# Decoder trunk on one core: the second attention's scores as three float32r products, its splits tied behind the copies, bias and maximum in one pass

## The chip, the core and the metric

The kernel runs on one core of a Trainium2 chip. The metric is device time in microseconds (us), the median of several executions; smaller is better. TensorE is called PE here (PEld is its weight load), VectorE DVE, ScalarE ACT, GpSimd POOL, and SP is the engine whose queue issues nearly all DMAs.

## The reference, cut to what matters

One sequence of 256 tokens, width 1024, 16 heads of 64. Layer 0 is a dilated sliding-window attention (three dilations), layer 1 is a forgetting attention, each followed by a SwiGLU block with a hidden width of 2816; all in float32. The change is mostly in the forgetting attention:

```
q, k, v, log_f = split(h @ w_in)          # log_f: one forget gate per head and token
c = cumsum(log_sigmoid(log_f + b_f))      # along the sequence
s = (q @ k.T) * 64 ** -0.5 + c_i - c_j    # per head, queries in two blocks of 128
s = where(key <= query, s, -1e30)
o = softmax(s) @ v
out = o @ w_out
```

## The kernel before

**Big products.** Every float32 weight and activation is split into two float32r halves: a high half made by a copy on ACT (`split`, line 74) and a low half made by a subtraction on DVE (line 78). `mm3` (lines 197 and 202) then forms a product as high x high, high x low and low x high, three float32r matmuls into one PSUM bank. Weights come in pieces: `piece` loads 128x2048 floats in two raw tiles of 128x1024 (five such buffers, issued on SP at line 95), and each raw tile costs one ACT copy (tile `wh`) and one DVE subtraction (tile `wl`). `weights(nm, i)` emits the pieces up to two ahead of the one that it returns; a raw buffer is free again when both of its halves are made.

**Order.** The program is written out as one long list. The framework orders each engine's queue ahead of time, by priority and by its own model of when inputs are ready; `first()` raises the priority of what is inside, and `tc.issue_after(ins)` places an instruction behind `ins` in its engine's queue. At run time each engine takes its queue strictly in order, and waits on semaphores.

**First attention.** The loop over `a_units` makes q and k of each dilation by `proj_feat`, and `rotated` (lines 433 to 436) turns them on DVE: a shuffle, a product with `rcos` that is the last read of the PSUM bank (line 434, returned as `read`), a product with `rsin`, a sum. In unit 2, before `rotated`, the code asks for `weights("a_in", 1)`, computes half of the next unit ahead of time, and scales `rcos` and `rsin` (line 569).

**Second attention.** `b_units` lists 12 weight units: three values first, then for four head quads `hq` the units q (`w = 0`) and k (`w = 1`), and the last quad's values. The loop's iterations 3 to 11 run them. Iteration i asks for its weights, which emits the splits of the unit two further on; it runs `proj_feat` for two halves (`c = 0, 1`), 24 matmuls of 256 columns each; then ACT copies the result from PSUM to SBUF, scaled by 0.125 for q (line 939, tile `fb`). PSUM tiles come in pairs (tags `mm`, `sc`, `tr`, `o`, two banks each).

Hooks in `due` put the attention of a quad between the halves of later units. After the k unit of quad `hq` (iterations 4, 6, 8, 10), `scores_b(hq, 0)` runs after the first half of the next iteration and `scores_b(hq, 1)` after its second. For a pair of heads, each on its own 64 array rows (`own`), `scores_b` issues four plain float32 matmuls (line 855; two query blocks of 128 and 256 keys for each head), on DVE one addition of the bias (line 861, 384 columns a head) and two maxima (line 865, 128 and 256 columns), on ACT an exponential for each (line 283), then a reciprocal (line 870) and the scaling by it, on ACT (line 872) and DVE (line 873). `trans_b` transposes the result on PE and copies it on DVE (line 297); `pv_b` multiplies by the values (line 304). `bias` (lines 838 to 841) fetches a bias tile by DMA and adds the causal mask on POOL. The low halves of the pieces that iterations 3 and 5 emit are collected in `behind` and released behind the gate scan or the first scores' addition.

Of the kernel before, what the change touches and what calls it, by code (L numbers as in the profile page):

```python
# [31 lines left out]
def trunk(ctx: ExitStack, tc: tile.TileContext, T, out):  # L32
# [10 lines left out]
    def first():  # L43

        return tc.high_priority(offset=300)
# [22 lines left out]
    euler = cst.tile([P, 1], F32, name="euler")  # L68
    nc.gpsimd.memset(euler, math.e)

    def split(pair, view, src, early=True, after=None):
        hi, lo = pair
        with first() if early else nullcontext():
            a = nc.scalar.activation(view(hi), src, AF.Copy)  # L74

            def low(after=None):
                with tc.issue_after(after.ins) if after else nullcontext():
                    return nc.vector.tensor_tensor(view(lo), src, view(hi).bitcast(F32), op=ALU.subtract)  # L78

            if isinstance(after, list):  # L80
                return after.append(low)
            return a, low(after)


    def piece(key, todo=None):
        if key[0][:2] == "dn" and key[1] == LATE:
            wh, wl = (y.rearrange("p k c -> p (k c)") for y in fm_tile("ot", KT, 1))
        else:
            wh, wl = (wp.tile([P, WIDE], F32R, tag=y, name=y, bufs=4) for y in ("wh", "wl"))
        if key == GATED:  # L90
            wh, wl = (y.rearrange("p (k c) -> p k c", k=KT) for y in (wh, wl))
        for c in range(2):
            raw = wp.tile([P, 1024], F32, tag="raw", name="raw", bufs=5)
            u = slice(c * 1024, (c + 1) * 1024)
            nc.sync.dma_start(raw, T[key[0]][key[1]][:, u])
            view = lambda y, u=u: y[:, u]
            if key == GATED:
                raw = raw.rearrange("p (k c) -> p k c", c=256)
                view = lambda y, c=c: y[:, c * 4:c * 4 + 4, :256]
            cut = lambda after=None, raw=raw, view=view: split((wh, wl), view, raw, False, after)  # L100
            if todo is None:
                cut()
            else:
                todo.append(cut)
        if key == GATED:
            cut = lambda after=None: split((wh, wl), lambda y: y[:, :, 256:], wf32, False, after)
            todo.append(cut)
        return wh, wl

# [35 lines left out]
    ready = {}  # L145
    state = {"next": 0}

    def weights(nm, i, after=None, ahead=AHEAD):

        upto = order.index((nm, i)) + ahead  # L150
        while state["next"] <= min(upto, len(order) - 1):
            key = order[state["next"]]
            cuts = []
            ready[key] = piece(key, cuts)
            for cut in cuts:
                cut(after)
            state["next"] += 1
        return ready.pop((nm, i))

# [122 lines left out]
    def exps(s, nm, den, j):  # L282
        nc.scalar.activation(s, s, AF.Exp, bias=nm[:, j:j + 1], accum_out=den[:, j:j + 1])
# [5 lines left out]
    def transposed(blocks, copy=nc.vector.tensor_copy, tag="tr"):  # L289

        tr = psum(tag)
        for i, b in enumerate(blocks):
            nc.tensor.transpose(tr[:, i * P:(i + 1) * P], b, ident)  # L293
        n = len(blocks) * P
        w = ap.tile([P, 512], F32, tag="pt", name="pt", bufs=3)
        with first():
            copy(w[:, :n], tr[:, :n])
        return w

    def pv(o, v, kb, pr, w, n, start, stop):  # L300

# [223 lines left out]
    def later(i, fn, *a):  # L525
        due.setdefault(i, []).append((fn, a))

    quads = [{"hq": hq, "fm": {}, "pt": {}, "v": {}} for hq in range(4)]
    for i, (hq, g, w) in enumerate(a_units):
        quad = quads[hq]  # L530
        if i == 3:
            o = o_next
        elif i:

            wt = weights("a_in", hq * 9 + g * 3 + w, read if i > 4 else None)
        if i != 3 and (w < 2 or g == 0 and hq > 1):
            o = psum("mm")
        if i == 1:
            ident = const("ident", [P, P])
            rcos = const("rcos", [P, S])  # L540
            rsin = const("rsin", [P, S])
        if i == 2:
            mask0 = const("mask0", [P, 3 * P])
            mask12 = const("mask12", [P, S])
        if i in (24, 31):
            x.append(hrow("x"))
            t = len(x) - 1
            nc.sync.dma_start(x[t], T["x"][t * P:(t + 1) * P, :])
        if w < 2:
            for c in range(2):  # L550
                if i == 3 and c == 0:
                    continue
                proj_feat(xt, wt, o[:, c * S:(c + 1) * S], c, (KT // 2, rstd_a) if i == 2 and c == 1 else None)
            if i == 2:
                values_12(quad["v"], lead)

                wt = weights("a_in", 1)
                o_next = psum("mm")
                rb = psum("tr")

                def rows():
                    for t in range(2):
                        nc.tensor.matmul(rb[:, t * P:(t + 1) * P], r_a[t].to_broadcast([P, P]), ident,
                                         start=True, stop=True)

                proj_feat(xt, wt, o_next[:, :S], 0, (6, rows))
                with first():
                    for c in (rcos, rsin):
                        nc.vector.tensor_tensor(c, c, rb[:, :S], op=ALU.mult)
            q, read = rotated(o, g, w)  # L570
            quad["fm"][g, w] = q
            if w == 1:

                j = i + (hq == 0)
                if g == 0:
                    for pr in range(2):
                        later(j + 2 + pr, scores_a, quad, g, pr)
                else:
                    later(j + 3 - g, scores_a, quad, g)
                if g == 2:  # L580
                    later(j + 1, softmax_a, quad)
                    j = 9 * hq + 11 + 2 * (hq == 0)
                    for pr in range(2):
                        later(j + pr, trans_a, quad, pr)
                        later(j + 1 + pr, pv_a, quad, pr)
        elif g == 0 and hq > 1:
            for t in range(2):
                proj_tok(xt, wt, o[:, t * S:(t + 1) * S], t)
            quad["v"][0] = v_tile(o, r_a)
        elif i > 1:  # L590


            half = hq % 2 if g == 0 else g - 1
            if half == 0:

                lead = [psum("mm" if g else "o") for _ in range(2)]
            proj_pair(xt, wt, lead, half)
            if half and g == 0:
                vs = [v_tile() for _ in range(2)]
                for t in range(2):  # L600
                    v_pair(vs, lead[t], t, r_a[t])
                for y in range(2):
                    quads[hq - 1 + y]["v"][0] = vs[y]
            elif half:
                values_12(quad["v"], lead)
        for fn, a in due.pop(i, ()):
            fn(*a)
# [239 lines left out]
    def scores_b(hq, pr):  # L847
# [3 lines left out]
        pt = b.setdefault("pt", {})  # L851
        scs = [psum("sc") for _ in range(2)]
        for qb in range(2):
            for h in range(2):
                last = nc.tensor.matmul(scs[h][:, qb * P:qb * P + (qb + 1) * P], b[0][own[h], pr, qb * P:(qb + 1) * P],  # L855
                                        b[1][own[h], pr, :(qb + 1) * P], start=True, stop=True)
        for h in range(2):
            s = p_tile()
            with first():
                bias_h = b["bias", pr][:, h * 3 * P:(h + 1) * 3 * P]  # L860
                added = nc.vector.tensor_tensor(s[:, :3 * P], scs[h][:, :3 * P], bias_h, op=ALU.add)
            for qb in range(2):
                j = h * 2 + qb
                sv = s[:, qb * P:qb * P + (qb + 1) * P]
                nc.vector.tensor_reduce(nm[:, j:j + 1], sv, axis=AX.X, op=ALU.max, negate=True)
                exps(sv, nm, den, j)
            pt[pr, h] = s
        release(added)
        c = stat_tile("c_b", 4)
# [49 lines left out]
    for hq in range(2):  # L919
        for pr in range(2):  # L920
            later(3 + 2 * hq, bias, hq, pr)
    for i, (hq, w) in enumerate(b_units):
        if i < 3:
            continue
        wt = weights("b_in", hq * 3 + w, behind if i in (3, 5) else None)
        o = psum("mm")
        if w < 2:
            for c in range(2):
# [4 lines left out]
            if w == 0:  # L933

                for fn, a in due.pop(i, ()):
                    fn(*a)
            bq[hq][w] = ap.tile([P, 2, S], F32, tag=f"fm{w}", name=f"fb{w}", bufs=2)
            with first():
                nc.scalar.activation(bq[hq][w], o.rearrange("p (a b) -> p a b", a=2), AF.Copy, scale=(0.125, 1.0)[w])
            if w == 1:  # L940
                j = i + 1

# [150 lines left out]
```

## Time and profile before

| | |
|---|---|
| median of 3 runs | 751.36 us (750.59 to 751.94) |
| the profiled execution | 752.26 us |
| its span, and what lies around it | 750.5 us, 1.76 us |
| granted TensorE clock | 0.997 |
| busy DVE, ACT, POOL | 500.7, 373.7, 67.3 us |
| bytes read by DMA | 136.07 MB, 183 GB/s over the span |

The second attention's loop lies at about 467 to 535 us of the span. In the lines of the profile, a group's row gives line, engine, operation, tiles, shape and count, then the total busy time in us and the mean of one instruction in ns, then the idle time of the engine before them. A timeline row gives start and duration in us; several instructions in a row are merged, and their number stands behind the x. A PE duration contains the pipeline's fill, so the pace of matmuls is read from start to start.

### The profile page before, as it was taken

How to read it: one execution, taken by the hardware profiler on the slowest of the kernel's cores; microseconds unless marked ns; L12 is line 12 of the kernel's file. 1: busy time of each engine (PE TensorE's matmuls, PEld its weight loads, DVE VectorE, ACT ScalarE, POOL GpSimd, SP SyncE). 2: the span in 40 equal slices, each digit the busy share in tenths (PEclk: the TensorE clock that was granted, in tenths of full speed). 3: DMA queues.
4: the chain of work that ended last, by engine and by line, in shares of the span. 5: the costliest groups of instructions: out<-in, count | busy, mean ns of one | idle time of the engine just before them, and what ended most of it. 6: DMA issues, size and time to landing. Idle time of an engine off the chain costs nothing.

```text
span 750.5 us, 14329 instructions
## 1 busy us (share of the span) xinstructions
PE 740.2 (99%) x5916; PEld 680.1 (91%) x5916; DVE 500.7 (67%) x752; ACT 373.7 (50%) x617; POOL 67.3 (9%) x98
## 2 busy tenths in 40 slices
PE   9999999999999999999999999999999999999996
PEld 7998989999998789999999988989889999999995
DVE  6987978876879376554556365799867545456533
ACT  7635537437427365444445355467556444445521
POOL 0600004004004000000000004312000000000001
PEclk9999999999999999999999999999999999999998
DMA  9865544645646267656567543784537665656601
GB/s 332 302 195 170 169 142 156 210 142 169 198 133 200 88 225 242 204 179 205 181 198 250 169 129 127 268 252 155 166 95 235 217 205 179 199 193 213 210 1 56
DMA packets 39441, 138.07 MB, mean 184 GB/s; under 512 B 4528, under 2 KB 5840, under 8 KB 39376
## 3 DMA queue, kind: packets, MB, share of 16 engines
q1 hardware_dynamic: 39232, 137.01, 55.3%
q8 instruction: 46, 0.75, 0.4%
q14 instruction: 19, 0.16, 0.1%
q10 hardware_dynamic: 144, 0.15, 0.1%
HBM read 136.07 MB, written 1.07 MB: 183 GB/s over the span
## 4 chain that ended last, share of the span: by engine, by line
PE 93%; ACT 2%; DVE 2%; DMA 2%; issue 1%; SPq 0%; POOL 0%; POOLq 0%; DVEq 0%; ACTq 0%
PE ps_mm L202 32%; PE ps_mm L197 17%; PE ps_tr L202 9%; PE ps_sc L202 8%; PE ps_o L202 7%; PE ps_tr L197 5%; PE ps_sc L197 4%; PE ps_o L197 4%; PE ps_o L304 2%; PE ps_tr L293 1%; DMA otl<-in_lead 1%; PE ps_sc L450 1%; PE ps_sc L466 1%; PE ps_sc L855 1%; ACT wh L74 1%; DMA raw<-in_a_in 1%
## 5 line engine op out<-in xcount | busy, mean ns | idle before, releaser
L74 ACT ACTIVATE wh<-raw 128x1024 fp32r<-128x1024 f32 x236 | 243.0, 1054 | 247.5 <-PE ps_mm L202 85.8
L78 DVE TENSOR_TENSOR wl<-raw,wh 128x1024 fp32r<-128x1024 f32 x236 | 287.7, 1238 | 81.8 <-ACT wh L74 81.5
L197 PE MATMUL ps_mm<-xt,wh 128*128 128x256 f32 x816 | 228.2, 280 | 0.7 <-DVE qk L434 0.7
L202 PE MATMUL ps_mm<-xt,wl 128*128 128x256 f32 x816 | 226.3, 277 | 0.1
L202 PE MATMUL ps_mm<-xt,wh 128*128 128x256 f32 x816 | 226.2, 277 | 0.0
L197 PEld LDWEIGHTS ps_mm<-xt,wh 128*128 128x128 f32 x816 | 153.3, 188 | 4.4 <-issue 3.3
L202 PEld LDWEIGHTS ps_mm<-xt,wl 128*128 128x128 f32 x816 | 153.4, 188 | 0.5 <-DVE wl L78 0.5
L202 PEld LDWEIGHTS ps_mm<-xt,wh 128*128 128x128 f32 x816 | 153.7, 188 | 0.0
L202 PE MATMUL ps_tr<-xt,wl 128*128 128x256 f32 x304 | 83.9, 276 | 0.0
L202 PE MATMUL ps_tr<-xt,wh 128*128 128x256 f32 x304 | 83.9, 276 | 0.0
L197 PE MATMUL ps_tr<-xt,wh 128*128 128x256 f32 x304 | 83.7, 276 | 0.0
L692 DVE TENSOR_TENSOR sa<-ps_tr,sa 128x256 f32<-128x256 f32 x38 | 16.1, 424 | 74.1 <-PE ps_tr L202 74.0
L202 PEld LDWEIGHTS ps_tr<-xt,wl 128*128 128x128 f32 x304 | 57.1, 188 | 0.0
L202 PEld LDWEIGHTS ps_tr<-xt,wh 128*128 128x128 f32 x304 | 57.1, 188 | 0.0
L197 PEld LDWEIGHTS ps_tr<-xt,wh 128*128 128x128 f32 x304 | 56.9, 188 | 0.0
L279 POOL COPY v<-v 32x256 f32<-32x256 f32 x64 | 36.1, 563 | 180.3 <-ACT v L275 177.6
L197 PE MATMUL ps_mm<-wh,xt 128*128 128x512 f32 (+1 forms) x144 | 50.1, 348 | 0.0
L202 PE MATMUL ps_mm<-wl,xt 128*128 128x512 f32 (+1 forms) x149 | 49.3, 336 | 0.0
L202 PE MATMUL ps_mm<-wh,xt 128*128 128x512 f32 (+1 forms) x149 | 49.2, 335 | 0.0
L167 POOL TENSOR_SCALAR rs<-ssq 128x1 f32<-128x1 f32 x7 | 2.1, 307 | 425.2 <-ACT junk L176 425.2
L197 PE MATMUL ps_sc<-wh,ah 128*128 128x512 f32 x80 | 31.4, 392 | 0.0
L202 PE MATMUL ps_sc<-wl,ah 128*128 128x512 f32 (+1 forms) x82 | 31.3, 385 | 0.0
(224 smaller groups left out, 1112.9 us busy)
## 6 DMA issues: line engine op xcount, KB each, us to landing
raw<-in_gu SPq DMA_DIRECT2D x88, 512.0 KB, 4.8
raw<-in_a_in SPq DMA_DIRECT2D x68, 512.0 KB, 4.4
raw<-in_dn SPq DMA_DIRECT2D x44, 512.0 KB, 4.5
raw<-in_b_in SPq DMA_DIRECT2D x24, 512.0 KB, 5.0
raw<-in_a_out SPq DMA_DIRECT2D x8, 512.0 KB, 4.5
raw<-in_b_out SPq DMA_DIRECT2D x8, 512.0 KB, 4.9
bias<-sums SPq DMA_DIRECT2D x8, 384.0 KB, 6.3
grow<-in_norms SPq DMA_DIRECT2D x4, 512.0 KB, 5.4
```

The costliest lines, as they stand in the source:

```text
L74: a = nc.scalar.activation(view(hi), src, AF.Copy)
L78: return nc.vector.tensor_tensor(view(lo), src, view(hi).bitcast(F32), op=ALU.subtract)
L167: nc.gpsimd.tensor_scalar(m, s, rest, None, op0=ALU.add)
L197: nc.tensor.matmul(o, sh, mh, start=start, stop=False)
L202: last = nc.tensor.matmul(o[:, u], s, m[:, u], start=False, stop=end and u.stop == n)
L279: nc.gpsimd.tensor_copy(v[1 + a % 2][n:n + 32, a // 2 * S:a // 2 * S + S], by_t[a * 32:a * 32 + 32, t, g])
L293: nc.tensor.transpose(tr[:, i * P:(i + 1) * P], b, ident)
L304: nc.tensor.matmul(o[h * HD:(h + 1) * HD], v[:, c:c + HD], w(h), start=start, stop=stop)
L450: nc.tensor.matmul(scs[h][:, qb * P:qb * P + (qb + 1) * P], q[hr[h], pr, qb * P:(qb + 1) * P], k[hr[h], pr, :(qb + 1) * P], start=True, st ...
L466: nc.tensor.matmul(sc[h][c, o:o + 64], q[hr[h], pq, qb * P + a * 32:qb * P + a * 32 + 32], k[hr[h], pq].rearrange("p (b n) -> p b n", b=2) ...
L692: nc.vector.tensor_tensor(a, u, sg, op=ALU.mult)
L855: last = nc.tensor.matmul(scs[h][:, qb * P:qb * P + (qb + 1) * P], b[0][own[h], pr, qb * P:(qb + 1) * P], b[1][own[h], pr, :(qb + 1) * P], ...
```

## The change

It does four things.

1. `scores_b` takes q and k as pairs of float32r halves. The ACT copy after each q and k unit now writes the high half; a new DVE instruction (`scalar_tensor_tensor`, 128x512, from PSUM and the high half) writes the low half into a tile `low` of the tag `h`. Each of the four score products becomes three float32r matmuls over 64 rows (high x high, high x low, low x high), alternating between the two heads.
2. The addition of the bias and the two maxima of a head become two `tensor_tensor_reduce`, of 128 and 256 columns, which write the negated sum and its minimum; the exponential runs with scale -1.
3. The pieces that iteration i of the second attention's loop emits are tied, in ACT's and DVE's queues, behind the ACT copy and the DVE low half of iteration i - 1 (`held`).
4. In unit 2 of the first attention, the second of the two low halves of `weights("a_in", 1)` is tied behind `read` of that unit's `rotated`.

```diff
+    def behind_(ins):
+        return tc.issue_after(ins.ins) if ins else nullcontext()
+
-    def split(pair, view, src, early=True, after=None):
+    def split(pair, view, src, early=True, after=None, hold=None):
         hi, lo = pair
         with first() if early else nullcontext():
-            a = nc.scalar.activation(view(hi), src, AF.Copy)
+            with behind_(hold and hold[0]):
+                a = nc.scalar.activation(view(hi), src, AF.Copy)
...
             if isinstance(after, list):
                 return after.append(low)
-            return a, low(after)
+            return a, low(after or hold and hold[1])
...
-    def weights(nm, i, after=None, ahead=AHEAD):
+    def weights(nm, i, after=None, ahead=AHEAD, hold=None):
...
-                cut(after)
+                cut(after, hold)
...
+    PRODUCTS = ((0, 0), (0, 1), (1, 0))
...
-                wt = weights("a_in", 1)
+                second = []
+                wt = weights("a_in", 1, second)
+                second.pop(0)()
...
             q, read = rotated(o, g, w)
+            if i == 2:
+                second.pop()(read)
...
         for qb in range(2):
-            for h in range(2):
-                last = nc.tensor.matmul(scs[h][:, qb * P:qb * P + (qb + 1) * P], b[0][own[h], pr, qb * P:(qb + 1) * P],
-                                        b[1][own[h], pr, :(qb + 1) * P], start=True, stop=True)
+            for i, (y, z) in enumerate(PRODUCTS):
+                for h in range(2):
+                    last = nc.tensor.matmul(scs[h][:, qb * P:qb * P + (qb + 1) * P],
+                                            b[0][y][own[h], pr, qb * P:(qb + 1) * P],
+                                            b[1][z][own[h], pr, :(qb + 1) * P], start=i == 0, stop=i == 2)
         for h in range(2):
             s = p_tile()
-            with first():
-                bias_h = b["bias", pr][:, h * 3 * P:(h + 1) * 3 * P]
-                added = nc.vector.tensor_tensor(s[:, :3 * P], scs[h][:, :3 * P], bias_h, op=ALU.add)
+            bias_h = b["bias", pr][:, h * 3 * P:(h + 1) * 3 * P]
             for qb in range(2):
-                j = h * 2 + qb
-                sv = s[:, qb * P:qb * P + (qb + 1) * P]
-                nc.vector.tensor_reduce(nm[:, j:j + 1], sv, axis=AX.X, op=ALU.max, negate=True)
-                exps(sv, nm, den, j)
+                j, u = h * 2 + qb, slice(qb * P, qb * P + (qb + 1) * P)
+                with first():
+                    added = nc.vector.tensor_tensor_reduce(s[:, u], scs[h][:, u], bias_h[:, u], -1.0, -NEG, ALU.add,
+                                                           ALU.min, nm[:, j:j + 1])
+                nc.scalar.activation(s[:, u], s[:, u], AF.Exp, bias=nm[:, j:j + 1], scale=-1.0,
+                                     accum_out=den[:, j:j + 1])
...
+    held = None
     for i, (hq, w) in enumerate(b_units):
...
-        wt = weights("b_in", hq * 3 + w, behind if i in (3, 5) else None)
+        wt = weights("b_in", hq * 3 + w, behind if i in (3, 5) else None, hold=held)
...
-            bq[hq][w] = ap.tile([P, 2, S], F32, tag=f"fm{w}", name=f"fb{w}", bufs=2)
+            if w == 0:
+                low = ap.tile([P, 2, 2, S], F32R, tag="h", name="fl", bufs=4)
+            ov = o.rearrange("p (a b) -> p a b", a=2)
+            qk = ap.tile([P, 2, S], F32R, tag=f"fm{w}", name=f"fb{w}", bufs=2)
+            bq[hq][w] = qk, low[:, w]
+            c = (0.125, 1.0)[w]
             with first():
-                nc.scalar.activation(bq[hq][w], o.rearrange("p (a b) -> p a b", a=2), AF.Copy, scale=(0.125, 1.0)[w])
+                held = (nc.scalar.activation(qk, ov, AF.Copy, scale=c),
+                        nc.vector.scalar_tensor_tensor(low[:, w], ov, c, qk.bitcast(F32), op0=ALU.mult,
+                                                       op1=ALU.subtract))
```

More of the change, by code (lines that the diff above doesn't have):

```diff
@@ L99, in piece @@
                 view = lambda y, c=c: y[:, c * 4:c * 4 + 4, :256]
-            cut = lambda after=None, raw=raw, view=view: split((wh, wl), view, raw, False, after)
+            cut = lambda after=None, hold=None, raw=raw, view=view: split((wh, wl), view, raw, False, after, hold)
             if todo is None:
@@ L105, in piece @@
         if key == GATED:
-            cut = lambda after=None: split((wh, wl), lambda y: y[:, :, 256:], wf32, False, after)
+            cut = lambda after=None, hold=None: split((wh, wl), lambda y: y[:, :, 256:], wf32, False, after, hold)
             todo.append(cut)
```

## The prediction

> **What bounds the kernel.** I read the page's busy times first, then PE's list of waits, then the timelines around its waits.
>
> ```profile
> PE 740.2 (99%) x5916; PEld 680.1 (91%) x5916; DVE 500.7 (67%) x752; ACT 373.7 (50%) x617; POOL 67.3 (9%) x98
> ```
>
> ```profile
> PE ps_sc L855 <- ACT fb L939: 1.6, 1, 1.6
> PE ps_o L313 <- DVE mhalf L65: 0.9, 1, 0.9
> PE ps_mm L197 <- DVE qk L434: 0.7, 1, 0.7
> ```
>
> PE works for 99% of the span, and its list has only three waits. So the time changes by what PE is given to do, by these waits, and by new ones; a faster DVE or ACT is worth nothing by itself. The change touches the first and the third wait and replaces one small group of PE's work. Here is the third, PE and then DVE:
>
> ```profile
> 29.07 0.28 PE L202 MATMUL ps_mm<-xt,wl 128*128 128x256 f32 x1
> 30.05 0.36 PE L197 MATMUL ps_mm<-xt,wh 128*128 128x256 f32 x1 [0.71 <-DVE qk L434]
> ```
>
> ```profile
> 26.37 0.74 DVE L433 STREAM_SHUFFLE rt<-ps_mm 128x512 f32<-128x512 f32 x1
> 27.32 1.33 DVE L78 TENSOR_TENSOR wl<-raw,wh 128x1024 fp32r<-128x1024 f32 x1 [0.21 <-ACT wh L74]
> 28.57 0.41 DVE L569 TENSOR_TENSOR rcos<-rcos,ps_tr 128x256 f32<-128x256 f32 x1
> 28.90 0.41 DVE L569 TENSOR_TENSOR rsin<-rsin,ps_tr 128x256 f32<-128x256 f32 x1
> 29.23 0.68 DVE L434 TENSOR_TENSOR qk<-ps_mm,rcos 128x512 f32<-128x512 f32 x1
> ```
>
> A weight split stands between the shuffle and the three instructions that PE's next bank waits for. The first wait of the list, PE and then ACT:
>
> ```profile
> 493.97 0.28 PE L202 MATMUL ps_mm<-xt,wl 128*128 128x256 f32 x1
> 495.88 0.93 PE L855 MATMUL ps_sc<-fb,fb 64*128 64x128 f32 x8 [1.63 <-ACT fb L939]
> ```
>
> ```profile
> 492.77 1.05 ACT L74 ACTIVATE wh<-raw 128x1024 fp32r<-128x1024 f32 x1
> 493.72 0.68 ACT L872 ACTIVATE p<-p,c_b 128x128 f32<-128x128 f32 x2
> 494.30 1.04 ACT L74 ACTIVATE wh<-raw 128x1024 fp32r<-128x1024 f32 x1
> 495.25 0.58 ACT L939 ACTIVATE fb<-ps_mm 128x512 f32<-128x512 f32 x1
> ```
>
> The second quad's scores wait for the copy of their k, and that copy stands behind splits of units that PE needs only later.
>
> **The early split.** PE's gap is 30.05 - 29.07 = 0.98, and its regular step 0.11 (480.84 to 480.96 in a fence below shows the same 0.12), so 0.87 is lost. With the split behind line 434, the scalings can follow the shuffle at about 27.1 and line 434 starts 29.23 - 28.57 = 0.66 later, at 27.8, and ends at 28.5, before PE's last matmul at 29.07. The wait goes whole unless `rb` is late by over 0.5. Behind the moved split stand only lines 435, 436 and the next unit's shuffle; DVE does the same sum of work up to that unit's line 434, and PE's list shows no wait there. Term: -0.87, between -0.87 and 0.
>
> **The products.** One call before, then the same call cut off after its first pair and its third pair of passes, then the loads:
>
> ```profile
> 480.84 0.28 PE L202 MATMUL ps_mm<-xt,wh 128*128 128x256 f32 x1
> 480.96 0.28 PE L202 MATMUL ps_mm<-xt,wl 128*128 128x256 f32 x1
> 481.16 0.93 PE L855 MATMUL ps_sc<-fb,fb 64*128 64x128 f32 x8
> 482.02 0.39 PE L197 MATMUL ps_mm<-xt,wh 128*128 128x256 f32 x1
> ```
>
> ```profile
> 481.16 0.38 PE L855 MATMUL ps_sc<-fb,fb 64*128 64x128 f32 x2
> ```
>
> ```profile
> 481.16 0.71 PE L855 MATMUL ps_sc<-fb,fb 64*128 64x128 f32 x6
> ```
>
> ```profile
> L304 PEld LDWEIGHTS ps_o<-pt,v 128*64 128x64 f32 x256 | 12.4, 137 | 5.1 <-issue 1.4 <-DVE pt L297 0.3 <-DVE nm_b L865 0.3
> ...
> L855 PEld LDWEIGHTS ps_sc<-fb,fb 64*128 64x128 f32 x64 | 4.2, 186 | 2.7 <-ACT fb L939 1.8
> ```
>
> A plain float32 product runs as two passes, and the two heads' passes run together: eight matmuls end 0.38, 0.71 (two pairs on) and 0.93 after the start. The last wide pair costs 0.22, so the second narrow one 0.33 - 0.22 = 0.11: 128 columns take 0.11 a pass, 256 take 0.22. From start to the next product's start a call takes 0.86: 0.66 for two narrow and two wide pairs, and 0.20 for entering the 64-row form and leaving it. The new call has three narrow and three wide pairs. A wide float32r matmul takes 0.11 (480.84 to 480.96). A narrow one needs at most the same, and its 128-column load bounds it below: loads of 64 and 128 columns take 137 and 186, so 49 for 64 columns and some 98 for 128. I take 0.11 for all six: 0.66, as before, plus 0.03 for two more pairs' issue. Eight calls: +0.2. The bounds: if the load hid behind the other head's stream, a narrow pair would take half a wide one, 0.055, and 24 of them save 1.3; if a narrow float32r matmul went at the plain float32 price, two passes or 0.22, 24 would cost 2.6 more. I stand by the middle since every 128-column pass in these rows carries a load and none is under 0.11.
>
> [...]
>
> **The second wait, and the tie.** The gap 493.97 to 495.88 is 1.91; an undisturbed entry takes 0.20 (480.96 to 481.16), so 1.7 is lost. Counting the splits along ACT's queue, the one at 494.30 is the first of unit (3, 0), which iteration 7 emits: it is now tied behind this very copy, 1.0 less. The one at 492.77 belongs to unit (2, 1), emitted by iteration 6 and tied only behind iteration 5's copy: it may stay in front. The other 0.7 is left to the softmax ahead of it, by these groups:
>
> ```profile
> L861 DVE TENSOR_TENSOR p<-ps_sc,bias 128x384 f32<-128x384 f32 x16 | 8.1, 545 | 4.2 <-PE ps_sc L855 4.2
> ...
> L78 DVE TENSOR_TENSOR xt<-ps_tr,xt 128x512 fp32r<-128x512 f32 x12 | 7.7, 681 | 1.5 <-ACT xt L74 1.5
> ...
> L865 DVE TENSOR_REDUCE nm_b<-p 128x1 f32<-128x256 f32 x16 | 6.5, 406 | 0.0
> ...
> L283 ACT ACTIVATE p<-p,nm_b 128x128 f32<-128x128 f32 x16 | 6.3, 394 | 13.3 <-DVE nm_b L865 13.3
> ...
> L865 DVE TENSOR_REDUCE nm_b<-p 128x1 f32<-128x128 f32 x16 | 4.3, 270 | 0.0
> ```
>
> ACT idled 13.3 for the maxima. A head costs DVE 0.545 + 0.406 + 0.270 = 1.22 now. The fused pass covers the same 384 columns in two instructions: 0.545 and one more fixed part, 0.270 - (0.406 - 0.270) = 0.13, so 0.68; no row shows `tensor_tensor_reduce`, and its bounds are 0.545 and the present 1.22. Two heads of a call end some 1.1 earlier, which covers the 0.7 on ACT. Against it stands the new low half: 128x512 from PSUM, 0.68 by the row of `xt`, behind the copy on a DVE that is full:
>
> ```profile
> 496.00:512.00 16.00, 16.00 (x142) 14.62 (x142) 15.96 (x30) 12.17 (x31) 3.32 (x3) 1.00 0.79 247
> ```
>
> (Third figure behind the span: DVE, 15.96 of 16.) Its sum stays level: 16 heads save 16 x 0.54 = 8.6, eight low halves cost 5.4. I leave 0.3 of the 1.7. Term: -1.4, between -1.7 and +0.7 (nothing gained, and the low half added).
>
> **The other three k.** Their copies were just in time, and the low half lengthens the chain by 0.68:
>
> ```profile
> 479.26 1.06 ACT L74 ACTIVATE wh<-raw 128x1024 fp32r<-128x1024 f32 x1 [2.54 <-DMA raw<-in_b_in]
> 480.23 0.58 ACT L939 ACTIVATE fb<-ps_mm 128x512 f32<-128x512 f32 x1
> ```
>
> ```profile
> 511.06 0.57 ACT L939 ACTIVATE fb<-ps_mm 128x512 f32<-128x512 f32 x1
> ```
>
> ```profile
> 511.93 0.93 PE L855 MATMUL ps_sc<-fb,fb 64*128 64x128 f32 x8
> ```
>
> The second pair of products needs the low half about 0.2 after the call's start: at 481.36 and 512.13. Left where they are, the copies would give it at 480.23 + 1.26 = 481.49 and 512.32, waits of 0.13 and 0.19 even on a free DVE. The tie moves the copy: the split at 479.26, which itself waited for its DMA, now goes behind the first k (iteration 5 emits it), so that copy can start when PE ends the unit, 24 steps or 2.7 before 481.16. I take +0.2 for the three together, between 0 and 2.4 (each behind most of a split). What is tied later is not missed: iteration i's pieces are used two units on, over 11 us later (a unit is 48 steps), and raw buffers that come free later delay SP's loads by no more than the tie's few us.
>
> **The sum.** -0.87 + 0.2 - 1.4 + 0.2 = -1.9. Against the profiled execution, 752.26 (span 750.5 and 1.76 around it): 750.4. That execution is 0.9 over the median of 751.36, which gives 749.5. 0.2%, about what a measurement of this kernel tells from no change, is 1.5.
>
> **The rivals.** *Narrow products at the plain float32 price:* +2.6 in place of +0.2, sum +0.5, 751.9: no change. For it: no row shows a float32r matmul under 256 columns. Against: the wide ones run at half a plain pass. *Low halves late (slower):* DVE in 496 to 512 is full, a queue in strict order, and a split at 1.2 ahead of a low half holds PE at line 855. If all four k meet most of one, the 1.7 stays with 0.7 on top and the others take 2.4: -0.87 + 0.2 + 0.7 + 2.4 = +2.4, 753.8. It decides from 2.4 of waits at the four calls in all: then the 0.87 and the 1.7, less 0.2 for the products, are eaten. Against: the low half has raised priority and the tie names it. *Heads one after the other:* if float32r products of two row halves don't run together, 48 more steps of 0.11, +5.3 in place of 0.2: 754.6. Against: the plain ones do. *Loads hidden:* -1.3 in place of +0.2: 748.0.
>
> **The numbers.** Forecast 0.47 (its own range 748.6 to 750.6), narrow price 0.24, late low halves 0.13, heads apart 0.05, loads hidden 0.11. Over 0.2% faster: two thirds of the forecast, the loads, a little of the others: 0.44. Slower: most of the late halves, the heads apart, the narrow price with a wait added: 0.18. The range runs from near the hidden loads to near the late halves, 748.2 to 753.2.
>
> **What would show it.** In the new profile: no PE wait for line 434 at 29 us; line 855's group from start to the next start 0.86 to 0.9 (1.2 would be the narrow price, 0.7 the hidden loads, 1.5 the heads apart); no wait for the copies over 0.3, and the new low half as a releaser of PE at most 0.5 in all; the fused pass near 0.68 a head. Over 1 us of waits on the low half, or a call of 1.2, makes the forecast wrong.

## The result, and the profile after

| | before | after |
|---|---|---|
| median of 11 runs each, same chip | 751.74 us | 749.48 us |
| lowest to highest | 750.59 to 754.20 | 748.84 to 750.78 |
| the profiled execution, its span | 752.26, 750.5 | 749.48, 747.7 |
| granted TensorE clock | 0.997 | 0.998 |

The ratio is 0.9972, with a 95% interval of 0.9964 to 0.9980: faster by 2.1 us, between 1.5 and 2.7. The forecast was 749.5, a gain of 1.9.

The page's busy times, then PE's list of waits, all of it, after the change:

```profile
PE 739.2 (99%) x5948; PEld 681.2 (91%) x5948; DVE 496.8 (66%) x776; ACT 375.0 (50%) x617; POOL 66.5 (9%) x98
```

```profile
PE ps_o L320 <- DVE mhalf L65: 0.9, 1, 0.9
PE ps_tr L298 <- DVE p L886: 0.6, 1, 0.6
```

The two waits that the change aims at are gone. One new wait has come, for the scaled scores `p` at line 298 (the transposes). Lines have moved: 197 and 202 are now 202 and 207 (`mm3`), 74 and 78 are 79 and 83 (`split`), 434 is 441, the scores' 855 is 867, the copy's 939 is 958, and the new low half is 959.

**The early wait.** PE where it waited, then DVE:

```profile
29.03 0.28 PE L207 MATMUL ps_mm<-xt,wl 128*128 128x256 f32 x1
29.15 0.28 PE L202 MATMUL ps_mm<-xt,wh 128*128 128x256 f32 x1
```

```profile
26.58 0.76 DVE L440 STREAM_SHUFFLE rt<-ps_mm 128x512 f32<-128x512 f32 x1
...
27.87 0.68 DVE L441 TENSOR_TENSOR qk<-ps_mm,rcos 128x512 f32<-128x512 f32 x1
...
29.11 1.42 DVE L83 TENSOR_TENSOR wl<-raw,wh 128x1024 fp32r<-128x1024 f32 x1
```

The bank is free when line 441 ends, at 28.55, and PE goes on at 29.15 with its regular step of 0.12. The split runs behind, at 29.11.

**One call of the scores**, on PE:

```profile
479.59 0.33 PE L867 MATMUL ps_sc<-fb,fb 64*128 64x128 f32 x2
...
479.87 0.28 PE L867 MATMUL ps_sc<-fb,fl 64*128 64x128 f32 x2
479.98 0.33 PE L867 MATMUL ps_sc<-fb,fb 64*128 64x256 f32 x2
...
480.47 0.38 PE L202 MATMUL ps_mm<-xt,wh 128*128 128x256 f32 x1
```

From start to the next product's start it is 480.47 - 479.59 = 0.88, against 0.86 before. A narrow pair steps by 479.98 - 479.87 = 0.11, as forecast for both widths.

**The second quad's k**, on ACT, and its low half on DVE:

```profile
491.01 0.58 ACT L958 ACTIVATE fb<-ps_mm 128x512 fp32r<-128x512 f32 x1
491.49 1.05 ACT L79 ACTIVATE wh<-raw 128x1024 fp32r<-128x1024 f32 x1
```

```profile
492.12 0.68 DVE L959 SCALAR_TENSOR_TENSOR fl<-ps_mm,fb 128x512 fp32r<-128x512 f32 x1
```

The split that stood right ahead of the copy now stands behind it. The low half ends at 492.80; PE started that call at 492.67 without a wait, and its second pair, the first to need the low half, 0.18 later, against 0.16 in the call above.

**DVE in the loop**, groups from 455 to 546 us, kept apart by shape:

```profile
L876 DVE CUSTOM_DVE_ANT_0 p<-ps_sc,bias 128x256 f32<-128x256 f32 x16 | 6.7, 418 | 0.0
...
L959 DVE SCALAR_TENSOR_TENSOR fl<-ps_mm,fb 128x512 fp32r<-128x512 f32 x8 | 5.5, 688 | 4.3 <-ACT fb L958 4.3
...
L876 DVE CUSTOM_DVE_ANT_0 p<-ps_sc,bias 128x128 f32<-128x128 f32 x16 | 4.5, 284 | 2.5 <-POOL bias L852 2.5
...
L876 DVE DVE_READ_ACCUMULATOR2_ANT nm_b<- 128x1 f32 x32 | 2.6, 82 | 0.0
```

The fused pass (it shows as a custom instruction) costs 0.418 + 0.284 = 0.70 a head, against 1.22 before. The read of its accumulator, 82 ns, starts together with the next instruction (in the last quad both at 533.30), so it adds nothing that shows.

**The new wait**, PE and then DVE:

```profile
535.37 0.82 PE L298 MATMUL ps_tr<-ident,p 128*128 128x128 f32 x6
536.80 0.59 PE L298 MATMUL ps_tr<-ident,p 128*128 128x128 f32 x2 [0.62 <-DVE p L886]
```

```profile
531.95 1.22 DVE L83 TENSOR_TENSOR wl<-raw,wh 128x1024 fp32r<-128x1024 f32 x1 [0.55 <-ACT wh L79]
533.10 0.28 DVE L876 CUSTOM_DVE_ANT_0 p<-ps_sc,bias 128x128 f32<-128x128 f32 x1
...
535.05 1.22 DVE L83 TENSOR_TENSOR wl<-raw,wh 128x1024 fp32r<-128x1024 f32 x1
...
536.39 0.62 DVE L886 TENSOR_SCALAR p<-p,c_b 128x256 f32<-128x256 f32 x2
```

Some 0.8 is lost there. The last quad's second pair of heads is late because DVE takes a split at 531.95, after idling 0.55 for that split's high half, ahead of the fused pass, and another at 535.05 ahead of the reciprocal. Both belong to pieces of the output projection (`out_proj`). Those are emitted behind the loop, where nothing ties them.

**Where the 2 us lie.** PE does the same 5852 matmuls in both kernels besides the scores. So I took the time between the same two matmuls in every profile. *Early* runs from the matmul that starts at 24.97 in the profile before to the one at 30.95, *loop* from the one at 469.95 to the one at 544.97. Changes are the measured ratio times the median of the kernel before on the same chip; they differ from the plain difference of the two medians by up to 0.4, and by 0.9 in the version without the tie. The versions ran on more than one chip, so changes are compared here rather than times; "single" is one execution.

| kernel | early | loop | time, us | change, us (95%) |
|---|---|---|---|---|
| before | 5.98 | 75.03 | 751.74 | |
| before, again | 6.10 | 74.35 | 751.01 | single |
| after | 5.01 | 74.08 | 749.48 | -2.1 (-2.7 to -1.5) |
| after, again | 5.16 | 74.49 | 750.28 | single |
| early split alone | 5.01 | 74.45 | 749.90 | -2.0 (-2.7 to -1.1) |
| early split alone, again | 5.01 | 74.85 | 749.62 | single |
| tie alone | 5.57 | 74.07 | 751.16 | -0.5 (-1.1 to +0.2) |
| fused pass alone | 6.13 | 74.73 | 751.38 | -0.1 (-0.8 to +0.6) |
| after, without the tie | 5.01 | 81.73 | 756.51 | +4.2 (+3.2 to +5.3) |
| after, addition and maxima apart | 5.01 | 78.89 | 754.37 | +2.8 (+2.0 to +3.7) |
| after, plain float32 scores | 5.01 | 73.29 | 748.66 | -3.1 (-4.1 to -2.0) |
| after, output splits tied | 5.00 | 73.22 | 748.42 | -3.3 (-4.2 to -2.3) |
| after, all products wide | 5.01 | 73.47 | 748.53 | -3.3 (-4.3 to -2.4) |
| before, no mask additions | 6.65 | 73.29 | 750.23 | -1.1 (-1.9 to -0.5) |

The early stretch is 1.0 shorter in all profiles with the early split but one (some 0.9 there). The loop is 0.4 shorter by the means of two profiles each (74.7 and 74.3). Outside these stretches the profiles agree within 1.6 us in sum, in places that change from execution to execution.

### The profile page after: what moved, and what is told of

It reads as the page before. It is cut to its first block, busy times and chain, and to the rows that moved or that the text cites. A ratio compares the mean times of both kernels' runs of the same rounds, so it can differ in the third digit from the quotient of the medians.

```text
span 747.7 us, 14417 instructions
## 1 busy us (share of the span) xinstructions
PE 739.2 (99%) x5948; PEld 681.2 (91%) x5948; DVE 496.8 (66%) x776; ACT 375.0 (50%) x617; POOL 66.5 (9%) x98
## 4 chain that ended last, share of the span: by engine, by line
PE 94%; DVE 2%; ACT 2%; DMA 1%; issue 1%; SPq 0%; POOL 0%; POOLq 0%; DVEq 0%; ACTq 0%
PE ps_mm L207 33%; PE ps_mm L202 17%; PE ps_tr L207 9%; PE ps_sc L207 8%; PE ps_o L207 7%; PE ps_tr L202 5%; PE ps_sc L202 4%; PE ps_o L202 4%; PE ps_o L311 2%; PE ps_tr L298 1%; DMA otl<-in_lead 1%; PE ps_sc L457 1%; PE ps_sc L473 1%; PE ps_sc L867 1%; PE ps_tr L195 1%; ACT wh L79 1%
## 5 line engine op out<-in xcount | busy, mean ns | idle before, releaser
L79 ACT ACTIVATE wh<-raw 128x1024 fp32r<-128x1024 f32 x236 | 242.6, 1054 | 243.7 <-PE ps_mm L207 74.7
```

## The experiments

### The change taken apart: early split alone

```diff
-                wt = weights("a_in", 1)
+                second = []
+                wt = weights("a_in", 1, second)
+                second.pop(0)()
...
+            if i == 2:
+                second.pop()(read)
```

> The kernel before with the early split alone moved. Waits theory: PE's gap at 29 us (0.98 from start to start, 0.87 of it a wait) goes, nothing else changes, the wait of 1.7 at 494 us stays: -0.87, about 0.9988 of before. Rival (the moved split only moves the wait): a new PE wait of 0.5 to 0.9 within the next 20 us, time unchanged.

It measured 749.90 against 751.61, ratio 0.9974 (0.9964 to 0.9985). From PE's list of waits:

```profile
...
PE ps_sc L859 <- ACT fb L943: 0.9, 1, 0.9
...
```

The early wait is gone, as said. The gain of 2.0 (1.7 by the plain difference of the medians) is larger than the 1.0 of the early stretch, and the interval, 1.1 to 2.7, leaves 0.87 out. DVE's order differs from the one before by this one split alone, and ACT's not at all. The second wait is still there, smaller than in the first profile: was that by the edit or by chance? Two further executions tell.

### The kernel before and the early split, each once more

Both kernels unchanged.

> The kernel before again, for its waits. Waits theory with a collision in it (the wait at 494 us hangs on whether the scaling at line 873 meets a POOL bias addition): PE's waits at 29 us and at line 855 differ from the first profile by up to 0.8, and line 873 has one instruction of about 1.4 us if the second wait is near 1.7, none if it is near 0.9. Rival (the schedule alone sets it): both waits within 0.1 of the first profile.

> The early move alone again. Collision theory: no wait at 29 us, and the wait at line 859 again anywhere between 0.7 and 1.8, larger if a scaling on DVE meets a POOL addition. Rival (the early move itself halves the second wait): 0.9 within 0.1 again.

The kernel before, again (751.01), and the early split alone, again (749.62):

```profile
...
PE ps_sc L855 <- ACT fb L939: 0.9, 1, 0.9
PE ps_mm L197 <- DVE qk L434: 0.8, 1, 0.8
```

```profile
PE ps_sc L859 <- ACT fb L943: 1.3, 2, 1.1
...
```

With PE's regular step put in, the second wait loses 1.7 and 0.97 in the two profiles before, 0.94 and 1.2 in the two with the early split. It varies from execution to execution, and the early split doesn't take it. So the 1.7 on which the prediction built was the largest of four values. What makes it vary is shown below, under the mask additions.

### Tie alone

```diff
+            with behind_(hold):
+                a = nc.scalar.activation(view(hi), src, AF.Copy)
...
-        wt = weights("b_in", hq * 3 + w, behind if i in (3, 5) else None)
+        wt = weights("b_in", hq * 3 + w, behind if i in (3, 5) else None, hold=held)
...
+                held = nc.scalar.activation(bq[hq][w], o.rearrange("p (a b) -> p a b", a=2), AF.Copy, scale=(0.125, 1.0)[w])
```

> The kernel before with only the ACT copies of the splits tied behind the q and k copies; plain float32 scores, separate addition and maxima, no early move. Waits theory: the k copy of the second quad loses the split in front of it, so PE's wait of 1.7 at 494 us falls to about 0.7; -1.0, about 0.9987. Rival (the fused pass did it, the tie is idle): the wait stays at 1.7, time unchanged. Second rival (the tie does all): the wait goes whole, -1.7.

Only ACT's half of the tie is in this version; there are no low halves of q and k to tie DVE's splits behind.

751.16, ratio 0.9994 (0.9986 to 1.0003). PE's waits:

```profile
...
PE ps_o L298 <- ACT p L877: 0.3, 1, 0.3
PE ps_sc L860 <- ACT fb L945: 0.3, 1, 0.3
...
```

The second wait is down to 0.4, and a wait of about 0.7 comes at the transposes of the last quad, at 538 us. So the tie gives back some 45 us later a part of what it gains, or all of it when measured from the 0.97 of the second profile before. The change of -0.5 is not clear of noise; -1.0 was expected. The early wait happened to be smaller in this profile (5.57 in the table).

### Fused pass alone

```diff
-                added = nc.vector.tensor_tensor(s[:, :3 * P], scs[h][:, :3 * P], bias_h, op=ALU.add)
...
-                nc.vector.tensor_reduce(nm[:, j:j + 1], sv, axis=AX.X, op=ALU.max, negate=True)
...
+                    added = nc.vector.tensor_tensor_reduce(s[:, u], scs[h][:, u], bias_h[:, u], -1.0, -NEG, ALU.add,
+                                                           ALU.min, nm[:, j:j + 1])
```

> The kernel before with only the fused pass of bias and maximum. Waits theory: two heads of a call end 1.1 us earlier on DVE, so the wait of 1.7 at 494 us falls by about 0.7 to 1.0; -0.9. Rival (the tie did it): wait unchanged, time unchanged. Second rival (the pass does all): the wait goes whole, -1.7.

751.38, ratio 0.9999 (0.9990 to 1.0008). PE's waits:

```profile
...
PE ps_mm L197 <- DVE qk L434: 0.9, 1, 0.9
PE ps_sc L855 <- ACT fb L939: 0.4, 1, 0.4
PE ps_sc L855 <- DVE nm_b L863: 0.2, 1, 0.2
...
```

The second wait falls to 0.5. One call at 499 us starts 0.3 late and takes 1.41 instead of 0.86, so 0.8 comes back there, and the -0.9 that was expected doesn't show. Each of the two edits by itself leaves 0.4 or 0.5 of the second wait, in one profile each; so they share it, and don't add up as 1.0 and 0.7.

### The change without the tie

```diff
-        wt = weights("b_in", hq * 3 + w, behind if i in (3, 5) else None, hold=held)
+        wt = weights("b_in", hq * 3 + w, behind if i in (3, 5) else None)
```

> The changed kernel without the tie: the splits of the second attention's loop may stand ahead of the copies and of the low halves. Waits theory: the copies of k come late again and the low half lengthens the chain, so PE waits at line 867 for one or more of the four k, 1 to 3 us in all; 1 to 3 us slower than the changed kernel, near before or slower. Rival (the fused pass alone removed the wait): same time as the changed kernel, -2.1 against before.

756.51, ratio 1.0056 (1.0042 to 1.0070), 6 to 7 slower than the change whole, where 1 to 3 was expected. PE's waits, then DVE ahead of the largest:

```profile
PE ps_sc L867 <- DVE fl L959: 3.3, 2, 2.5
PE ps_sc L867 <- ACT fb L958: 1.8, 1, 1.8
...
```

```profile
491.54 5.69 DVE L83 TENSOR_TENSOR wl<-raw,wh 128x1024 fp32r<-128x1024 f32 x4
497.15 0.68 DVE L959 SCALAR_TENSOR_TENSOR fl<-ps_mm,fb 128x512 fp32r<-128x512 f32 x1
```

Four splits in a row stand ahead of one low half: PE took the copy that it reads at 494.82, and the low half starts 2.3 later, behind the splits. This is the rival of the late low halves as the prediction drew it, and the tie, on ACT and DVE together, keeps it off. Its lack costs twice: PE loses about 5.8 by waiting, and then its clock falls. Windows of 1 us; the seventh figure behind the span is the granted clock:

```profile
495.00:496.00 1.00, 0.41 (x3) 0.15 (x3) 1.00 (x1) 0.87 (x1) 0.01 (x1) 0.93 0.83 234
...
502.00:503.00 1.00, 1.00 (x8) 1.00 (x7) 0.96 (x4) 0.30 (x1) 0.00 (x0) 0.65 1.10 411
```

The clock is 0.50 in the windows between these two. PE works from 497.88 to about 502.7 at half speed, which loses some 2.4. Waits and clock make 8.2; less the 0.8 to 1.3 that the change whole waits, 6.9 to 7.4, against 7.4 between the loop stretches (81.73 and the mean 74.3).

### The change with addition and maxima apart

The edit of the fused pass alone, taken back in the kernel after.

> The changed kernel with the addition and the two maxima apart again. Waits theory: DVE gets 16 x 0.54 us more work and the maxima come later; the k copy of the second quad is late by some 0.7, so a wait of 0.5 to 1.0 at about 492 us, and the last softmax is later too: 0.7 to 1.5 slower than the changed kernel. Rival (the tie alone suffices): within 0.3 of the changed kernel.

754.37, ratio 1.0037 (1.0026 to 1.0049), 4.9 slower than the change whole, where 0.7 to 1.5 was expected. PE's waits, and the windows in which the clock falls and comes back (it is 0.50 between them):

```profile
PE ps_o L298 <- ACT p L885: 1.8, 1, 1.8
PE ps_sc L867 <- ACT fb L958: 1.1, 1, 1.1
...
PE ps_sc L867 <- DVE fl L959: 0.8, 1, 0.8
```

```profile
494.00:495.00 1.00, 0.71 (x10) 0.64 (x10) 1.00 (x2) 1.00 (x2) 0.00 (x0) 0.97 0.91 324
...
498.00:499.00 1.00, 1.00 (x9) 1.00 (x9) 1.00 (x3) 0.00 (x0) 0.00 (x0) 0.82 0.68 213
```

About 4.2 of waits, and 3.4 us at half clock that lose 1.7: 5.9, less the 0.8 to 1.3, is 4.6 to 5.1, as measured. The fused pass, worth nothing alone, is what pays for the low halves' DVE time.

### The change with plain float32 products

```diff
...
+            for h in range(2):
+                last = nc.tensor.matmul(scs[h][:, qb * P:qb * P + (qb + 1) * P], b[0][own[h], pr, qb * P:(qb + 1) * P],
+                                        b[1][own[h], pr, :(qb + 1) * P], start=True, stop=True)
...
+                held = nc.scalar.activation(qk, ov, AF.Copy, scale=c), None
```

> The changed kernel with the scores as plain float32 products again and no low halves of q and k; fused pass, tie and early move stay. Waits theory: a call costs PE 0.86 in place of 0.88, and the DVE is lighter by 8 x 0.69: within 0.3 us of the changed kernel, -2.1 to -2.6 against before. Rival (the float32r products themselves save time on PE): slower than the changed kernel by about 1 us, -1.1 against before.

748.66, ratio 0.9959 (0.9945 to 0.9973). No wait in the loop is left, nor at the output projection, and a call is 0.86. So the float32r products buy no time: without them and their low halves the median is 0.8 lower (the intervals overlap; the loop stretch, 73.29 against 74.08 and 74.49, agrees). The expectation, within 0.3 of the changed kernel, missed this: it counted the lighter DVE but not the wait at the output projection, which this version doesn't have.

### All products 256 columns wide

```diff
-                    last = nc.tensor.matmul(scs[h][:, qb * P:qb * P + (qb + 1) * P],
+                    last = nc.tensor.matmul(scs[h][:, qb * S:(qb + 1) * S],
...
-                                            b[1][z][own[h], pr, :(qb + 1) * P], start=i == 0, stop=i == 2)
+                                            b[1][z][own[h], pr], start=i == 0, stop=i == 2)
...
-                    added = nc.vector.tensor_tensor_reduce(s[:, u], scs[h][:, u], bias_h[:, u], -1.0, -NEG, ALU.add,
+                    added = nc.vector.tensor_tensor_reduce(s[:, u], scs[h][:, qb * S:qb * S + (qb + 1) * P], bias_h[:, u], -1.0, -NEG, ALU.add,
```

> The changed kernel with every narrow product made wide: the first query block also multiplies the later 128 keys, whose results are never read. Load theory: a narrow pair of float32r products takes as long as its 128-column load, about 0.11, and a wide one takes 0.11, so a call costs 0.88 as before and the time is that of the changed kernel within 0.2. Rival (the narrow pair is cheaper than its load, 0.055): 24 pairs x 0.055 = 1.3 us slower than the changed kernel.

The call of the first k, on PE:

```profile
479.30 0.38 PE L867 MATMUL ps_sc<-fb,fb 64*128 64x256 f32 x2
...
480.21 0.38 PE L202 MATMUL ps_mm<-xt,wh 128*128 128x256 f32 x1
```

0.91 instead of 0.88: twice the columns in three of six pairs cost 0.03, 9 ns a pair. So a narrow pair's time is not that of its columns. Nor is it a fixed price of issuing two loads and two matmuls: the first attention, in the kernel before, has pairs of heads with loads of 64 columns and matmuls of 64 columns. Here they are on PE, the same stretch cut off after four pairs and after five:

```profile
98.00 0.40 PE L304 MATMUL ps_o<-pt,v 128*64 128x64 f32 x8
```

```profile
98.00 0.46 PE L304 MATMUL ps_o<-pt,v 128*64 128x64 f32 x10
```

Such a pair steps by 0.06. By elimination I put the 0.11 down to the load of 128 columns; no run varies the load alone. The kernel's time (748.53, ratio 0.9956, 0.9943 to 0.9968) isn't to be compared for this, and it missed the expected 0.2 around the changed kernel: its queues came out in another order, without the wait at the output projection.

### The new wait: real, and removed

The kernel after once more, unchanged:

> The changed kernel again, for its waits. Waits theory: no wait at 29 us or at line 867 over 0.3, the wait of the transposes at 536 us again between 0.4 and 1.2. Rival (the new wait was chance): no wait at 536 us.

The wait for `p` at line 298 is there again, 0.80 lost (750.28), and another 0.45 is lost to the second k's low half.

Then the low halves of the output projection's third and fourth pieces tied behind the last fused pass and the last scaling:

```diff
-    def out_proj(nm, ot, h, grow, done, banks):
+    def out_proj(nm, ot, h, grow, done, banks, holds=()):
...
-        ws = [weights(nm, i) for i in range(4)]
+        ws = [weights(nm, i, hold=(None, holds[i]) if i < len(holds) else None) for i in range(4)]
...
+        b["done"] = added, scaled
...
-    hs, xt = out_proj("b_out", ot, [h for h, _ in hs], g_f, 5, ("mm", "sc"))
+    hs, xt = out_proj("b_out", ot, [h for h, _ in hs], g_f, 5, ("mm", "sc"), bq[3]["done"])
```

> The changed kernel with two more ties: the low halves of the third output-projection piece behind the last fused pass, those of the fourth behind the last scaling on DVE. Waits theory: the new wait of the changed kernel (0.6 to 0.8 us at 536 us, transposes waiting for the last scaling behind two splits) goes, no other wait comes: -0.8 against the changed kernel, -2.9 against before. Rival (the moved splits are then late for the output projection): PE waits for a low half near 534 us by 0.5 to 1.5, no gain.

748.42, ratio 0.9956 (0.9944 to 0.9969): the lowest median here, 1.1 under the kernel after (the intervals of the two ratios just overlap) and level with the plain products. That fits a float32r cost that was mostly this wait. PE's list holds only the wait for `mhalf`, which every kernel here has. DVE's pass that came at 533.10 above:

```profile
530.41 0.29 DVE L876 CUSTOM_DVE_ANT_0 p<-ps_sc,bias 128x128 f32<-128x128 f32 x1 [1.29 <-issue]
```

The fused pass comes 2.7 earlier, and the wait is gone.

### What feeds the second wait: the mask additions on POOL

In the first profile before, DVE's splits and scalings took far longer in places than in others, always beside an addition of the mask on POOL (DVE, then POOL):

```profile
484.15 4.05 DVE L78 TENSOR_TENSOR wl<-raw,wh 128x1024 fp32r<-128x1024 f32 x2
...
489.31 1.72 DVE L873 TENSOR_SCALAR p<-p,c_b 128x256 f32<-128x256 f32 x2
```

```profile
483.59 3.52 POOL L841 TENSOR_TENSOR bias<-bias,causal 128x512 f32<-128x512 f32 x2 [0.87 <-DMA bias<-sums]
489.32 1.29 POOL L841 TENSOR_TENSOR bias<-bias,causal 128x512 f32<-128x512 f32 x1 [2.21 <-DVE c_b L870]
```

```diff
-        nc.gpsimd.tensor_tensor(d, d, causal[:, None, None, :].to_broadcast([P, 2, 2, P]), op=ALU.add)
```

> The kernel before without POOL's additions of the causal mask to the bias tiles (line 841); the scores of later keys are then not masked out, the rest is unchanged. Collision theory: the DVE splits of 1.8 to 2.3 us and the scaling of 1.4 us near 484 to 490 us fall to 1.2 and 0.35, DVE is some 2 us ahead, and PE's wait at 494 us falls to 0.7 or less: -1.0 or more against before. Rival (POOL costs DVE nothing that PE waits for): the wait stays at 1.7, time unchanged.

This version leaves the mask out; the order of all instructions on DVE and ACT stays that of the kernel before. 750.23, ratio 0.9985 (0.9975 to 0.9994). The same two groups, on DVE:

```profile
484.16 2.35 DVE L78 TENSOR_TENSOR wl<-raw,wh 128x1024 fp32r<-128x1024 f32 x2
...
488.21 0.61 DVE L872 TENSOR_SCALAR p<-p,c_b 128x256 f32<-128x256 f32 x2
```

PE's wait for the second k is gone without any edit to splits or softmax. DVE is 4.05 - 2.35 + 1.72 - 0.61 = 2.8 shorter ahead of it. The early wait, on the other hand, is longer here (6.65 in the table above); PE then waits for a high half made on ACT, which is itself behind a DMA.

The collisions also explain why the second wait varies. In the second profile before, the scalings came out shorter:

```profile
488.64 1.04 DVE L873 TENSOR_SCALAR p<-p,c_b 128x256 f32<-128x256 f32 x2
```

The same two groups on DVE, in the four profiles whose second attention is that of the kernel before, and without the mask, in us:

| profile | two splits | two scalings | sum | lost in the second wait |
|---|---|---|---|---|
| before | 4.05 | 1.72 | 5.77 | 1.7 |
| before, again | 3.97 | 1.04 | 5.01 | 0.97 |
| early split alone | 4.00 | 0.99 | 4.99 | 0.94 |
| early split alone, again | 4.07 | 1.20 | 5.27 | 1.2 |
| before, no mask additions | 2.35 | 0.61 | 2.96 | 0 |

In the first four rows the sum less the wait is 4.0 to 4.1: the wait follows the time of these two groups one for one, and without collisions the sum is 1.1 short of where it begins. So the wait before was the sum of splits in front of the copy, a long softmax, and these collisions; shortening any one takes most or all of it.

## Why the prediction was right, and where it was not

**The early split (-0.87).** Right: the wait goes whole, the early stretch is 1.0 shorter, and line 441 ends at 28.55 where 28.5 was forecast.

**The products (+0.2).** Right: a call is 0.88, 0.02 to 0.03 over before, and a narrow pair 0.11. The wide version shows that its columns don't bound it (9 ns a pair for twice as many), and the pairs with half the load at 0.06 that issuing doesn't; by elimination the load is left, which no run varies alone. The rival of the plain price would be a call of 1.2, that of the hidden loads 0.7, that of heads apart 1.5: none is seen. (The prediction puts each of these rivals in place of the +0.2, though its prices come on top of it; their sums are 0.2 too low, which changes no verdict.)

**The second wait (-1.4).** The mechanism was right, its size and its parts were not. The 1.7 was one profile's value; another has 0.97, and so the term could take only some 1.3. Its parts, 1.0 by the tie and 0.7 by the softmax, fail too: either alone brings the wait to 0.4 or 0.5. And a third cause was not foreseen, the collisions with POOL's mask additions: they set the size of the wait in each execution, and without them it is gone with neither edit.

**The other three k (+0.2).** No wait is lost there in the first profile after. What the term missed lies after the loop: the step failed that asked of the tied pieces alone whether they are missed, and not what the untied pieces of the next stage do once the loop's order has changed. They cost 0.8. With this, and with the second wait smaller than taken, the loop gives -0.4 (74.7 to 74.3, means of two profiles) where the terms of the loop made -1.0. That the whole came out near -1.9 is partly accident: the change gains more than the profiles account for, as follows.

**"A faster DVE is worth nothing by itself".** True of the fused pass alone, and misleading for the whole: without it the change is 4.9 slower.

**The rival of the late low halves.** Named rightly, with the right guard against it. It was priced at 1.7 + 0.7 + 2.4 = 4.8 of waits, a sum of +2.4. Without the tie the waits were 5.8, and the clock added 2.4 that no term had: +4.2 (3.2 to 5.3).

**What stays open.** The loop and the early stretch explain -1.4 of the -2.1, just outside its interval, and -1.0 or less of the early split's -2.0. (The profiled executions alone, two of each kernel, differ by 1.8.) Some 0.6 to 1 us more goes in the five versions with the early split that came out faster, and no wait accounts for it. The profiles contain stretches, many of them 15 us long or more, in which 256-column matmuls step by 0.118 instead of 0.113, at a granted clock of 1.00; one right behind the early wait, worth 0.6 to 0.8, is in two of the five profiles that have that wait and in none of the nine without. That would fit, but no experiment tested it. Why the plain and the wide version have no wait at the output projection wasn't tried apart either.

## What to carry to other kernels

When a change moves work within a strictly ordered queue, look one stage past the place that it aims at: the untied work there takes the slots that come free. A wait's size in one profile is one draw; profile the kernel twice before building a sum on it. An edit that is worth nothing alone can be what pays for another, so test by taking each out of the whole, not only by adding each to the start.

## What the runs showed of the hardware

**Waits and the clock.** PE's gaps in the version with addition and maxima apart:

```profile
491.79 0.28 PE L207 MATMUL ps_mm<-xt,wl 128*128 128x256 f32 x1
493.17 0.33 PE L867 MATMUL ps_sc<-fb,fb 64*128 64x128 f32 x2 [1.10 <-ACT fb L958]
494.29 0.33 PE L867 MATMUL ps_sc<-fl,fb 64*128 64x128 f32 x2 [0.80 <-DVE fl L959]
```

Two gaps, 1.38 and 1.12 from start to start, with a pair of matmuls between, and then the clock is halved from 494.94 (0.97 in that window is 0.06 us at half) to 498.36 (0.82, or 0.36 us): 3.42 us. Without the tie it is halved from 495.86 to 502.70, 6.84 us, twice that. A single gap of 1.9 in the kernel before left it at 1.00, and so did a single one of 2.2 later in this same run (539.38 to 541.54). So gaps of 1.38 and 1.12 close together were followed by a halved clock, and single ones of 1.9 and 2.2 were not. What decides it, and what sets the lengths of 3.42 and 6.84, the runs don't show.

**DVE against POOL.** Two splits, each with two SBUF inputs, take 2.35 without the mask additions and 4.05 beside them, two scalings 0.61 and 1.72. The addition of the bias, with one input in PSUM, takes 0.55 without and, in the first profile before, 0.56 beside one (at 482.18). Not every split beside a mask addition is long: in the first profile before, three of seven take the usual 1.2, while each split that takes over 1.3 and each scaling that takes over 0.4 in the loop overlaps one. Why some are slowed and others not, the runs don't show.
